# Packing the last layer's key ends over two heads, and giving GpSimd every fourth rest of the weights

## The chip, the cores and the metric

The kernel runs on one core of a Trainium2 chip. The metric is the device time of one execution in microseconds; lower is better. The same times are shown for several executions, and one execution was taken by the hardware profiler, whose trace is read below. Engines are written as in the profile: PE is TensorE's matmuls and PEld its weight loads, DVE is VectorE, ACT is ScalarE, POOL is GpSimd, SP is SyncE.

## The reference

Two transformer-like blocks for one sequence of 256 tokens and 2048 features, everything in float32. The first block is attention over compressed, selected and windowed keys beside a gated spatial unit. The second has 16 further tokens in front (272 in all) and two layers. Its even layer runs a state-space scan in both directions and a depthwise convolution of 31 taps over 2048 channels; its odd layer is neighbourhood attention on a grid:

```python
def even_layer(h, ...):
    u = rmsnorm(h, norm_g)
    z_a, xs, Bm, Cm, dt_f, dt_b, z_b, glu_v, glu_g = split(u @ w_in)
    y_a = ssd_mixer(xs, Bm, Cm, dt_f, dt_b, z_a, ...)        # conv of 5 taps, scan, gate, norm
    y_b = conformer_conv(glu_v, glu_g, ...) * silu(z_b)      # GLU, depthwise conv of 31 taps, layer norm
    return h + concat(y_a, y_b) @ w_out

def odd_layer(h, ...):
    q, k, v, z = split(rmsnorm(h, norm_g) @ w_in)
    # 32 heads of 64. A query sees 16 grid columns around its own and the 16 tokens in front
    o = softmax(q k^T / 8 + bias, masked) v
    return h + (o * silu(z)) @ w_out
```

## The kernel before

**Weights in two parts.** Products with weights keep float32's precision on a faster matmul form. `load_piece` (L89 to L101) fetches 1024 columns of weights (`raw`, on SP's queue). ACT rounds them to `wh` (L98), and DVE computes what is left, `wl = raw - wh` (L99). `raw`, `wh` and `wl` have four buffers each. Activations are split the same way, and `mm3` (L118 to L122) adds three products. `proj` (L137) makes one output block of 128 rows from 16 chunks, which are two pieces: 48 matmuls over 256 or 272 columns, 24 for each piece.

**The even layer** (`layer_e`, its projections from about 860 to 1555 us in the trace) makes 96 projections, in this order: 32 for the GLU, 16 for B and C, 16 for x, 16 for the gate z_a, 16 for z_b; of the GLU's, the first four need no split. DVE does the convolution: 480 taps, each one `scalar_tensor_tensor` on a whole channel block (L842), on SBUF alone. For 11 of the 16 blocks the taps read their inputs from the tile `early`, whose space is taken over, block by block, by `xt` when x is made; the taps on a part must be done before that. GpSimd adds the finished blocks (`vsum`, L849) and, later, the squares (L204). While B, C and x run, DVE also does the small convolution (`cacc`, L873, its input in PSUM) and then the decay tiles `m` of the scan (L904, on SBUF), which PE multiplies (`yps`, L940 and L956). DVE's gate products (`za`, L992) read PSUM.

**The odd layer** (`layer_o`) is a loop of 16 steps of two heads each: projections q, k, v and z; four transposes of v (L1154); scores for two tiles of 128 queries against 176 keys, with both heads side by side (`sp`, 352 columns); softmax on DVE and ACT; then, per tile, four transposes of the probabilities `pt_ps` (128 and 48 keys for each head, L1188 and L1189) and four products with the values (L1195, contracting 128 or 48 keys, 64 output rows for each head). Each of these products is two passes in the trace.

**What sets the order.** The program is handed to a scheduler with its own model of the engines; it puts each engine's instructions into one queue, worked off in order. `K.hook` (called at L100) and `tc.issue_after` tie taps behind the `wl` of a piece.

Of the kernel before, what the change touches and what calls it, by code (L numbers as in the profile page):

```python
# [10 lines left out]
F32 = mybir.dt.float32  # L11
# [34 lines left out]
class Core:  # L46


    def __init__(self, tc, ctx):
        self.tc, self.nc = tc, tc.nc  # L50
        nc = self.nc
        self.cp = ctx.enter_context(tc.tile_pool(name="const", bufs=1))
        self.wp = ctx.enter_context(tc.tile_pool(name="w", bufs=2))
        self.sm = ctx.enter_context(tc.tile_pool(name="small", bufs=4))
        self.ps = ctx.enter_context(tc.tile_pool(name="ps", bufs=3, space=PSUM))
        self.dr = ctx.enter_context(tc.tile_pool(name="dram", bufs=1, space=DRAM))
        self.hpool = ctx.enter_context(tc.tile_pool(name="h", bufs=1))
# [32 lines left out]
    def load_piece(self, src):  # L90
# [7 lines left out]
        nc.scalar.activation(wh, raw, AF.Copy)  # L98
        ins = nc.vector.tensor_tensor(wl, raw, wh.bitcast(F32), op=ALU.subtract)  # L99
        self.hook(ins.ins)  # L100
        return wh, wl  # L101
# [576 lines left out]
def layer_e(K, a):  # L678
# [3 lines left out]
    with ExitStack() as ctx:  # L682
# [55 lines left out]
        def glu():  # L738
# [354 lines left out]
def layer_o(K, a, out):  # L1093
# [4 lines left out]
    h = K.h  # L1098
    KR = [(0, 176), (96, T2)]
    VR = [(0, 128), (128, 176), (96, 224), (224, T2)]  # L1100
    with ExitStack() as ctx:
# [26 lines left out]
        for i in range(2):  # L1128
            nc.gpsimd.memset(kbd[i].bitcast(F32), 0.0)

        for i in range(16):
            bias = wk.tile([P, 2, 2, 176], F32, tag="bias", name="bias")
            nc.sync.dma_start(bias, a["rpb"][i])
# [14 lines left out]
            vp = K.proj(a["o_w_in"][4 * i + 2], UH, UL, T2)  # L1148
            vf = k1("vf")
            nc.vector.tensor_tensor(vf, vp, rb, op=ALU.mult)  # L1150
            vt_ps = K.ps.tile([P, 4, P], F32, tag="t", bufs=2, name="vt_ps")
            vt = wk.tile([P, 4, P], F32, tag="vt", name="vt")
            for j, (s0, s1) in enumerate(VR):
                nc.tensor.transpose(vt_ps[: s1 - s0, j, :], vf[:, s0:s1], K.ident)  # L1154
            nc.scalar.activation(vt[:, 0::2, :], vt_ps[:, 0::2, :], AF.Copy)
            nc.scalar.activation(vt[:48, 1::2, :], vt_ps[:48, 1::2, :], AF.Copy)
            zp = K.proj(a["o_w_in"][4 * i + 3], QH, QL, S)
# [8 lines left out]
            for t in range(2):  # L1166
                ts = slice(128 * t, 128 * t + 128)
                k0, k1_ = KR[t]
                K.mm3(sp[:, t, :352].rearrange("p (g k) -> p g k", g=2), qh[:, ts], ql[:, ts],
                      kb[:, 0, :, k0:k1_], kb[:, 1, :, k0:k1_], True, True)  # L1170
            sb = wk.tile([P, 2, 2, 176], F32, tag="sb", name="sb")
            nc.vector.tensor_tensor(sb.rearrange("p t g k -> p t (g k)"), sp[:, :, :352],
                                    bias.rearrange("p t g k -> p t (g k)"), op=ALU.add)
# [9 lines left out]
            for t in range(2):  # L1183
                ts = slice(128 * t, 128 * t + 128)
                pt_ps = K.ps.tile([P, 2, 2, P], F32, tag="t", bufs=2, name="pt_ps")
                for g in range(2):
                    nc.vector.tensor_scalar(sb[:, t, g], sb[:, t, g], rs[:, t, g : g + 1], None, op0=ALU.mult)
                    nc.tensor.transpose(pt_ps[:, 0, g, :], sb[:, t, g, 0:128], K.ident)  # L1188
                    nc.tensor.transpose(pt_ps[:48, 1, g, :], sb[:, t, g, 128:176], K.ident)  # L1189
                pt = wk.tile([P, 2, 2, P], F32, tag="pt", name="pt")  # L1190
                nc.scalar.activation(pt[:, 0], pt_ps[:, 0], AF.Copy)
                nc.scalar.activation(pt[:48, 1], pt_ps[:48, 1], AF.Copy)
                for kt, n in ((0, 128), (1, 48)):
                    for g in range(2):
                        nc.tensor.matmul(o_ps[64 * g : 64 * g + 64, ts], vt[:n, 2 * t + kt, 64 * g : 64 * g + 64], pt[:n, kt, g, :],  # L1195
                                         start=kt == 0, stop=kt == 1, skip_group_check=True)
            o = k1("oz", S)
# [51 lines left out]
def prep(inp):  # L1249
# [70 lines left out]
    rpb = g["o_rpb_2"][0]  # L1320
    bias = np.zeros((32, P, 2, 176), f32)
    for t, (q0, k0) in enumerate(((0, 0), (144, 96))):
        qr, qc = row[q0 : q0 + 128, None], col[q0 : q0 + 128, None]
        kr, kc = row[None, k0 : k0 + 176], col[None, k0 : k0 + 176]
        st = np.clip(qc - 8, 0, 48)
        ok = (kc >= st) & (kc < st + 16)
        b = rpb[:, np.clip(kr - qr + 7, 0, 14), np.clip(kc - qc + 15, 0, 30)]
        bias[:, :, t] = np.where(kc < 0, f32(0), np.where(ok, b, f32(-1e30)))
    o["rpb"] = np.ascontiguousarray(bias.reshape(16, 2, P, 2, 176).transpose(0, 2, 3, 1, 4))

# [49 lines left out]
```

## Time and profile before

| | us |
|---|---|
| median of 3 runs (lowest, highest) | 2284.5 (2283.99, 2286.28) |
| the profiled execution's own time | 2284.89 |
| its span in the trace | 2283.1 |
| PE busy | 2229.3 |
| DVE busy | 1628.3 |
| ACT busy | 1164.8 |
| POOL busy | 124.7 |

The span runs from the first to the last instruction; the execution's own time is 1.8 us longer. An engine's busy time is the union of its instructions. PE is busy 98% of the span, so the places of interest are those where it is not, and its own instructions where it is.

### The profile page before, as it was taken

The numbers are of one execution on the slowest core, as the hardware profiler recorded it, in microseconds if no ns is written. First come the engines' busy times: TensorE is split into PE (matmuls) and PEld (weight loads), VectorE is DVE, ScalarE is ACT, GpSimd is POOL, SyncE is SP. The second block draws the span as 40 slices with busy tenths as digits, with TensorE's granted clock in tenths as the row PEclk, the third lists the DMA queues.
The fourth block names the chain that finished last, engine by engine and source line by source line (L and its number), as shares of the span: only waits on it lengthen the run. The fifth ranks groups of instructions, "written<-read, shape, count | busy, mean of one in ns | idle before, by whom it ended". The sixth has DMA issues, their size and how long they took to land.

```text
span 2283.1 us, 44200 instructions
## 1 busy us (share of the span) xinstructions
PE 2229.3 (98%) x17798; PEld 2159.0 (95%) x17798; DVE 1628.3 (71%) x2840; ACT 1164.8 (51%) x2087; POOL 124.7 (5%) x119
## 2 busy tenths in 40 slices
PE   8999999999999999999998998899999999999997
PEld 6998799999999998999998998899999999999997
DVE  6567777555555669999999888798766555565554
ACT  4446644444444444445547887745444545454453
POOL 1000000000000130000000010002011000000011
PEclk9999999999999999999999999999999999999999
DMA  7642455555556555554554555354655555545453
GB/s 260 226 153 94 133 191 183 187 186 186 187 195 209 183 165 195 198 175 166 177 175 145 171 172 189 120 177 153 202 176 188 170 168 169 169 162 167 159 174 121
DMA packets 126413, 398.20 MB, mean 174 GB/s; under 512 B 16832, under 2 KB 33664, under 8 KB 125696
## 3 DMA queue, kind: packets, MB, share of 16 engines
q1 hardware_dynamic: 126064, 395.36, 52.5%
q8 instruction: 140, 2.29, 0.4%
q14 instruction: 65, 0.53, 0.1%
q10 hardware_dynamic: 144, 0.01, 0.0%
HBM read 390.92 MB, written 4.40 MB: 173 GB/s over the span
## 4 chain that ended last, share of the span: by engine, by line
PE 94%; DVE 3%; ACT 2%; issue 1%; DMA 0%; POOL 0%; SPq 0%; DVEq 0%; ACTq 0%; POOLq 0%
PE acc L120 29%; PE acc L122 28%; PE acc L121 28%; PE acc L156 2%; PE o_ps L1195 1%; PE yps L956 1%; DVE wl L99 1%; DVE vb L842 0%; PE pt_ps L503 0%; PE sp L120 0%; ACT wh L98 0%; PE sp L122 0%; PE sp L121 0%; PE o_ps L509 0%; DVE xin L291 0%
## 5 line engine op out<-in xcount | busy, mean ns | idle before, releaser
L98 ACT ACTIVATE wh<-raw 128x1024 fp32r<-128x1024 f32 x674 | 713.2, 1059 | 967.9 <-PE acc L121 575.6
L99 DVE TENSOR_TENSOR wl<-raw,wh 128x1024 fp32r<-128x1024 f32 x674 | 828.9, 1231 | 383.7 <-ACT wh L98 376.2
L120 PE MATMUL acc<-uh,wh 128*128 128x272 f32 (+1 forms) x1488 | 437.8, 294 | 15.7 <-DVE za L992 8.7
L122 PE MATMUL acc<-uh,wl 128*128 128x272 f32 (+1 forms) x1488 | 437.5, 294 | 0.0
L121 PE MATMUL acc<-ul,wh 128*128 128x272 f32 (+1 forms) x1488 | 435.1, 292 | 0.0
L121 PE MATMUL acc<-xl,wh 128*128 128x256 f32 (+1 forms) x1136 | 322.3, 284 | 0.0
L120 PE MATMUL acc<-xh,wh 128*128 128x256 f32 (+1 forms) x1136 | 322.2, 284 | 0.0
L122 PE MATMUL acc<-xh,wl 128*128 128x256 f32 (+1 forms) x1136 | 321.2, 283 | 0.0
L120 PEld LDWEIGHTS acc<-uh,wh 128*128 128x128 f32 (+1 forms) x1488 | 282.7, 190 | 21.5 <-DVE za L992 9.5
L121 PE MATMUL acc<-oul,wh 128*128 128x256 f32 (+1 forms) x1024 | 294.4, 287 | 0.0
L122 PE MATMUL acc<-ouh,wl 128*128 128x256 f32 (+1 forms) x1024 | 294.0, 287 | 0.0
L120 PE MATMUL acc<-ouh,wh 128*128 128x256 f32 (+1 forms) x1024 | 292.8, 286 | 0.0
L122 PEld LDWEIGHTS acc<-uh,wl 128*128 128x128 f32 (+1 forms) x1488 | 282.1, 190 | 3.5 <-issue 2.3
L121 PEld LDWEIGHTS acc<-ul,wh 128*128 128x128 f32 (+1 forms) x1488 | 282.4, 190 | 1.7 <-issue 0.8
L120 PEld LDWEIGHTS acc<-xh,wh 128*128 128x128 f32 (+1 forms) x1136 | 213.8, 188 | 1.2 <-DVE pj L316 0.4
L122 PEld LDWEIGHTS acc<-xh,wl 128*128 128x128 f32 (+1 forms) x1136 | 214.4, 189 | 0.2
L121 PEld LDWEIGHTS acc<-xl,wh 128*128 128x128 f32 (+1 forms) x1136 | 213.6, 188 | 0.7 <-issue 0.4
L122 PEld LDWEIGHTS acc<-ouh,wl 128*128 128x128 f32 x1024 | 192.6, 188 | 2.6 <-issue 2.6
L121 PEld LDWEIGHTS acc<-oul,wh 128*128 128x128 f32 x1024 | 192.7, 188 | 0.2
L120 PEld LDWEIGHTS acc<-ouh,wh 128*128 128x128 f32 x1024 | 192.8, 188 | 0.0
L842 DVE SCALAR_TENSOR_TENSOR vb<-early,par,vb 128x257 f32<-128x257 f32 (+9 forms) x330 | 148.4, 493 | 0.9 <-ACT vb L826 0.7
L204 POOL TENSOR_TENSOR sq<-sq 128x272 f32<-128x272 f32 (+1 forms) x44 | 48.5, 1103 | 747.5 <-ACT sq L201 746.7
(413 smaller groups left out, 4290.7 us busy)
## 6 DMA issues: line engine op xcount, KB each, us to landing
raw<-in_e_w_in SPq DMA_DIRECT2D x184, 512.0 KB, 4.0
raw<-in_w_in_fm SPq DMA_DIRECT2D x140, 512.0 KB, 3.9
raw<-in_o_w_in SPq DMA_DIRECT2D x128, 512.0 KB, 4.1
raw<-in_e_w_out SPq DMA_DIRECT2D x64, 512.0 KB, 4.5
raw<-in_w_up SPq DMA_DIRECT2D x32, 512.0 KB, 3.9
raw<-in_w_out SPq DMA_DIRECT2D x32, 512.0 KB, 4.4
raw<-in_w_pg SPq DMA_DIRECT2D x32, 512.0 KB, 3.8
raw<-in_o_w_out SPq DMA_DIRECT2D x32, 512.0 KB, 4.5
```

Source lines behind the costliest of these rows:

```text
L98: nc.scalar.activation(wh, raw, AF.Copy)
L99: ins = nc.vector.tensor_tensor(wl, raw, wh.bitcast(F32), op=ALU.subtract)
L120: mm(out, lh, rh, start=start, stop=False)
L121: mm(out, lh, rl, start=False, stop=False)
L122: mm(out, ll, rh, start=False, stop=stop)
L156: self.nc.tensor.matmul(a, raws[c // 8][:, c % 8, :], x(c), start=c == 0, stop=c == 15)
L204: self.nc.gpsimd.tensor_tensor(acc, acc, sq, op=ALU.add)
L842: ins = nc.vector.scalar_tensor_tensor(v[:, lo:hi], u[:, lo + o : hi + o], par(K, "e_dw_w", 31 * b + k), v[:, lo:hi], op0=ALU.mult, op1=AL ...
L956: prev = nc.tensor.matmul(o, w, m, start=False, stop=k >= 6, skip_group_check=True).ins
L1195: nc.tensor.matmul(o_ps[64 * g : 64 * g + 64, ts], vt[:n, 2 * t + kt, 64 * g : 64 * g + 64], pt[:n, kt, g, :], start=kt == 0, stop=kt == 1 ...
```

## The change

There are two independent parts.

1. **Even layer.** A counter of pieces and a `share` are added to the core. From the GLU's first projection to the end of z_b's `share` is 4, and every fourth piece's subtraction is issued to GpSimd in place of DVE. 46 pieces are concerned. The hook is then given the last subtraction that DVE did.
2. **Odd layer.** The two query tiles see 192 keys in place of 176, from 0 and from 80. Keys 128 columns wide are used for each head as its own part (from 0 for the first head and from 64 for the second), and the 64 that are left of each head are packed beside each other into one tile of 128. That makes three transposes of the probabilities per tile, and three products: one that contracts the packed tile for both heads at once (128 output rows, with a block-diagonal value tile `vb`), and one of 128 keys for each head. The scores are 384 columns wide.

```diff
@@ load_piece
         nc.scalar.activation(wh, raw, AF.Copy)
-        ins = nc.vector.tensor_tensor(wl, raw, wh.bitcast(F32), op=ALU.subtract)
-        self.hook(ins.ins)
+        self.pieces += 1
+        if self.share and self.pieces % self.share == 0:
+            nc.gpsimd.tensor_tensor(wl, raw, wh.bitcast(F32), op=ALU.subtract)
+        else:
+            self.last_wl = nc.vector.tensor_tensor(wl, raw, wh.bitcast(F32), op=ALU.subtract).ins
+        self.hook(self.last_wl)
@@ layer_e
+        K.share = 4
         early = big.tile([P, 3 * D], F32, tag="e6", name="early")
         us = [glu()]
...
         K.hook = lambda ins: None
+        K.share = 0
@@ layer_o
-    KR = [(0, 176), (96, T2)]
-    VR = [(0, 128), (128, 176), (96, 224), (224, T2)]
+    KR = [(0, 192), (80, T2)]
...
-            vf = k1("vf")
-            nc.vector.tensor_tensor(vf, vp, rb, op=ALU.mult)
+            vb = vbd[i % 2]
+            vf = k1("vf", 208)
+            for g in range(2):
+                gs = slice(64 * g, 64 * g + 64)
+                nc.vector.tensor_tensor(vf[gs], vp[gs, 64 * g : 64 * g + 208], rb[gs, 64 * g : 64 * g + 208], op=ALU.mult)
+                nc.vector.tensor_tensor(vb[gs, :, gs], two(vp[gs], 128 - 128 * g), two(rb[gs], 128 - 128 * g), op=ALU.mult)
...
-            for j, (s0, s1) in enumerate(VR):
-                nc.tensor.transpose(vt_ps[: s1 - s0, j, :], vf[:, s0:s1], K.ident)
-            nc.scalar.activation(vt[:, 0::2, :], vt_ps[:, 0::2, :], AF.Copy)
-            nc.scalar.activation(vt[:48, 1::2, :], vt_ps[:48, 1::2, :], AF.Copy)
+            for t, (k0, k1_) in enumerate(KR):
+                nc.tensor.transpose(vt_ps[:, 2 * t, :], vf[:, 80 * t : 80 * t + P], K.ident)
+                nc.tensor.transpose(vt_ps[:, 2 * t + 1, :], vb[:, t, :], K.ident)
+            nc.scalar.activation(vt, vt_ps, AF.Copy)
...
-                    nc.tensor.transpose(pt_ps[:, 0, g, :], sb[:, t, g, 0:128], K.ident)
-                    nc.tensor.transpose(pt_ps[:48, 1, g, :], sb[:, t, g, 128:176], K.ident)
-                pt = wk.tile([P, 2, 2, P], F32, tag="pt", name="pt")
-                nc.scalar.activation(pt[:, 0], pt_ps[:, 0], AF.Copy)
-                nc.scalar.activation(pt[:48, 1], pt_ps[:48, 1], AF.Copy)
-                for kt, n in ((0, 128), (1, 48)):
-                    for g in range(2):
-                        nc.tensor.matmul(o_ps[64 * g : 64 * g + 64, ts], vt[:n, 2 * t + kt, 64 * g : 64 * g + 64], pt[:n, kt, g, :],
-                                         start=kt == 0, stop=kt == 1, skip_group_check=True)
+                    nc.tensor.transpose(pt_ps[:, g, :], sb[:, t, g, 64 * g : 64 * g + P], K.ident)
+                nc.tensor.transpose(pt_ps[:, 2, :], sb[:, t].rearrange("p g k -> p (g k)")[:, 128:256], K.ident)
+                pt = wk.tile([P, 3, P], F32, tag="pt", name="pt")
+                nc.scalar.activation(pt, pt_ps[:, 0:3], AF.Copy)
+
+                nc.tensor.matmul(o_ps[:, ts], vt[:, 2 * t + 1, :], pt[:, 2, :], start=True, stop=False, skip_group_check=True)
+                for g in range(2):
+                    nc.tensor.matmul(o_ps[64 * g : 64 * g + 64, ts], vt[:, 2 * t, 64 * g : 64 * g + 64], pt[:, g, :],
+                                     start=False, stop=True, skip_group_check=True)
```

The bias tile and the tile `sb` grow from 176 to 192 keys, and two `vb` tiles are cleared on GpSimd at the layer's start.

The order of DVE in the GLU's stretch, before, from the 26th to the 29th piece after the first one that the change concerns (`wl` a piece's rest, `vb<-early` taps, `early<-gt,acc` a GLU output):

```order
L99 TENSOR_TENSOR wl<-raw,wh 128x1024
L842 SCALAR_TENSOR_TENSOR vb<-early,par,vb 128x258
L751 SCALAR_TENSOR_TENSOR early<-gt,acc 128x272
L842 SCALAR_TENSOR_TENSOR vb<-early,par,vb 128x257 x4
L99 TENSOR_TENSOR wl<-raw,wh 128x1024
L842 SCALAR_TENSOR_TENSOR vb<-early,par,vb 128x258 x2
L842 SCALAR_TENSOR_TENSOR vb<-early,par,vb 128x259
L99 TENSOR_TENSOR wl<-raw,wh 128x1024
L842 SCALAR_TENSOR_TENSOR vb<-early,par,vb 128x259
L842 SCALAR_TENSOR_TENSOR vb<-early,par,vb 128x260 x2
L842 SCALAR_TENSOR_TENSOR vb<-early,par,vb 128x261
L99 TENSOR_TENSOR wl<-raw,wh 128x1024
```

The same four pieces in the order after; the third of them is the moved one, between the second and the third `wl`:

```order
L104 TENSOR_TENSOR wl<-raw,wh 128x1024
L848 SCALAR_TENSOR_TENSOR vb<-early,par,vb 128x265
L756 SCALAR_TENSOR_TENSOR early<-gt,acc 128x272
L848 SCALAR_TENSOR_TENSOR vb<-early,par,vb 128x265
L848 SCALAR_TENSOR_TENSOR vb<-early,par,vb 128x266
L104 TENSOR_TENSOR wl<-raw,wh 128x1024
L848 SCALAR_TENSOR_TENSOR vb<-early,par,vb 128x266
L848 SCALAR_TENSOR_TENSOR vb<-early,par,vb 128x267 x2
L848 SCALAR_TENSOR_TENSOR vb<-early,par,vb 128x268 x2
L848 SCALAR_TENSOR_TENSOR vb<-early,par,vb 128x269 x2
L848 SCALAR_TENSOR_TENSOR vb<-early,par,vb 128x270 x2
L848 SCALAR_TENSOR_TENSOR vb<-early,par,vb 128x271 x2
```

Behind these rows stands the next `wl`. In the place of the moved `wl` stand taps, 11 between two rows of `wl` where there were three and four.

The order of POOL in the even layer, before (`vsum` the sum of finished convolution blocks, `sq` sums of squares, `tmp` the sum at the layer's end):

```order
L847 COPY vsum<-vb 128x272
L849 TENSOR_TENSOR vsum<-vsum,vb 128x272 x10
L204 TENSOR_TENSOR sq<-sq 128x272 x11
L849 TENSOR_TENSOR vsum<-vsum,vb 128x272 x2
L204 TENSOR_TENSOR sq<-sq 128x272 x4
L849 TENSOR_TENSOR vsum<-vsum,vb 128x272 x3
```

And after, the beginning of the same stretch:

```order
L102 TENSOR_TENSOR wl<-raw,wh 128x1024 x3
L853 COPY vsum<-vb 128x272
L102 TENSOR_TENSOR wl<-raw,wh 128x1024 x3
L855 TENSOR_TENSOR vsum<-vsum,vb 128x272 x2
L102 TENSOR_TENSOR wl<-raw,wh 128x1024 x4
L855 TENSOR_TENSOR vsum<-vsum,vb 128x272 x2
```

The moved pieces stand between the sums of `vsum`, which wait for taps; further on they stand between the sums of `sq` as well.

The order of PE in the odd layer's loop, before, the transposes of the probabilities between two projection matmuls:

```order
L120 MATMUL acc<-ouh,wh 128x272
L1188 MATMUL pt_ps<-ident,sb 128x128
L1189 MATMUL pt_ps<-ident,sb 48x128
L1188 MATMUL pt_ps<-ident,sb 128x128
L1189 MATMUL pt_ps<-ident,sb 48x128
L1188 MATMUL pt_ps<-ident,sb 128x128
L1189 MATMUL pt_ps<-ident,sb 48x128
L1188 MATMUL pt_ps<-ident,sb 128x128
L1189 MATMUL pt_ps<-ident,sb 48x128
```

After, the products with the values, which were eight of one form (`o_ps<-pt,vt 64x128 x8`):

```order
L126 MATMUL acc<-oul,wh 128x272
L1212 MATMUL o_ps<-pt,vt 128x128
L1214 MATMUL o_ps<-pt,vt 64x128 x2
L1212 MATMUL o_ps<-pt,vt 128x128
L1214 MATMUL o_ps<-pt,vt 64x128 x2
```

Their places among the projection's matmuls stay: 22 projection matmuls stand between the transposes and these products in both.

## Rows read from the trace of the kernel before

**Rows 1.** The page: busy time, share of the span, instructions, by engine.
```profile
PE 2229.3 (98%) x17798; PEld 2159.0 (95%) x17798; DVE 1628.3 (71%) x2840; ACT 1164.8 (51%) x2087; POOL 124.7 (5%) x119
```

**Rows 2.** Busy time by window: stretch, length, engines (instructions), granted PE clock, DMA.
```profile
core 0: us, PE busy (x) PEld busy (x) DVE busy (x) ACT busy (x) POOL busy (x), PEclk, DMA share, GB/s
900.00:1200.00 300.00, 300.00 (x2378) 298.43 (x2378) 285.77 (x507) 141.99 (x199) 6.94 (x9) 0.99 0.55 182
1200.00:1220.00 20.00, 17.44 (x137) 16.28 (x136) 20.00 (x48) 15.77 (x40) 0.00 (x0) 1.00 0.44 144
1220.00:1240.00 20.00, 15.00 (x101) 13.78 (x101) 17.22 (x33) 13.17 (x35) 1.60 (x2) 0.83 0.39 122
1227.40:1232.80 5.40, 5.37 (x24) 5.37 (x25) 4.82 (x12) 3.79 (x13) 0.00 (x0) 0.51 0.51 168
1241.00:1400.00 159.00, 157.06 (x1230) 148.17 (x1229) 132.96 (x273) 129.22 (x332) 9.69 (x10) 1.00 0.55 174
...
1777.00:1804.35 27.35, 27.35 (x228) 26.48 (x227) 16.15 (x25) 13.62 (x27) 0.00 (x0) 1.00 0.53 170
```

**Rows 3.** Waits (total us, times, longest) of 900 to 1200, then of 1200 to 1240.
```profile
ACT wh L98 <- PE acc L121: 102.3, 62, 2.0
...
DVE wl L99 <- ACT wh L98: 12.8, 40, 2.0
...
PE yps L956 <- DVE m L904: 5.8, 2, 4.1
```

**Rows 4.** The page's costliest groups (busy us, mean ns | idle before), then DVE's timeline.
```profile
L98 ACT ACTIVATE wh<-raw 128x1024 fp32r<-128x1024 f32 x674 | 713.2, 1059 | 967.9 <-PE acc L121 575.6
L99 DVE TENSOR_TENSOR wl<-raw,wh 128x1024 fp32r<-128x1024 f32 x674 | 828.9, 1231 | 383.7 <-ACT wh L98 376.2
...
1228.04 2.08 DVE L842 SCALAR_TENSOR_TENSOR vb<-u,par,vb 128x259 f32<-128x259 f32 x5
1230.05 0.43 DVE L880 SCALAR_TENSOR_TENSOR xs<-ct,cacc 128x272 f32<-128x272 f32 x1
```

**Rows 5.** Timeline (start, length) of DVE and POOL; L1083 by source, ns min/median/max.
```profile
1655.67 1.23 DVE L99 TENSOR_TENSOR wl<-raw,wh 128x1024 fp32r<-128x1024 f32 x1 [0.22 <-ACT wh L98]
1656.81 1.00 DVE L1083 SCALAR_TENSOR_TENSOR oul<-h,par,ouh 128x272 fp32r<-128x272 f32 x1
...
1656.44 1.07 POOL L1089 TENSOR_TENSOR tmp<-tmp,sq 128x272 f32<-128x272 f32 x1 [93.97 <-ACT sq L1088]
...
L1083 DVE SCALAR_TENSOR_TENSOR oul<-h,par,ouh x16: 494/1005/1011, 1650.7 to 1741.0; 128x272 fp32r<-128x272 f32 x16
```

**Rows 6.** L291 by source; timeline of POOL and of DVE beside it.
```profile
L291 DVE TENSOR_SCALAR xin<-xin,par x16: 340/350/1455, 4.4 to 23.1; 128x256 f32<-128x256 f32 x16
...
7.74 1.26 POOL L289 TENSOR_TENSOR sq<-sq,sq 128x512 f32<-128x512 f32 x1 [6.80 <-ACT sq L287]
...
1460.45 0.77 POOL L204 TENSOR_TENSOR sq<-sq 128x272 f32<-128x272 f32 x1 [15.48 <-ACT sq L201]
...
1460.62 0.44 DVE L992 SCALAR_TENSOR_TENSOR za<-zt,acc 128x272 f32<-128x272 f32 x1 [0.19 <-ACT zt L991]
```

**Rows 7.** Timeline of one step of the odd layer's loop, PE and (1798.18) DVE.
```profile
1791.21 0.33 PE L120 MATMUL sp<-kb,qh 128*128 128x352 f32 x1
1791.38 0.33 PE L121 MATMUL sp<-kb,qh 128*128 128x352 f32 x1
...
1798.18 0.97 DVE L1187 TENSOR_SCALAR sb<-sb,rs 128x176 f32<-128x176 f32 x4
...
1801.00 0.27 PE L1188 MATMUL pt_ps<-ident,sb 128*128 128x128 f32 x1
...
1801.76 0.27 PE L1189 MATMUL pt_ps<-ident,sb 128*48 128x128 f32 x1
...
1804.71 1.54 PE L1195 MATMUL o_ps<-pt,vt 128*64 128x128 f32 x16
1806.18 0.40 PE L122 MATMUL acc<-ouh,wl 128*128 128x272 f32 x1
```

More of the change, by code (lines that the diff above doesn't have):

```diff
@@ L60, in __init__ @@
         self.hook = lambda ins: None
+        self.share, self.pieces = 0, 0
         self.wide, self.wide_i, self.wide_t = False, 0, None
@@ L1129, in layer_o, with two @@
             nc.gpsimd.memset(kbd[i].bitcast(F32), 0.0)
+        vbd = [big.tile([P, 2, P], F32, tag="vb%d" % i, name="vb%d" % i) for i in range(2)]
+        for i in range(2):
+            nc.gpsimd.memset(vbd[i], 0.0)
+        def two(v, o):
+            v = v[:, o : o + 64]
+            return bass.AP(tensor=v.tensor, offset=v.offset, ap=[v.ap[0], [80, 2], [1, 64]])
         for i in range(16):
-            bias = wk.tile([P, 2, 2, 176], F32, tag="bias", name="bias")
+            bias = wk.tile([P, 2, 2, 192], F32, tag="bias", name="bias")
             nc.sync.dma_start(bias, a["rpb"][i])
@@ L1168, in layer_o @@
                 k0, k1_ = KR[t]
-                K.mm3(sp[:, t, :352].rearrange("p (g k) -> p g k", g=2), qh[:, ts], ql[:, ts],
+                K.mm3(sp[:, t, :384].rearrange("p (g k) -> p g k", g=2), qh[:, ts], ql[:, ts],
                       kb[:, 0, :, k0:k1_], kb[:, 1, :, k0:k1_], True, True)
-            sb = wk.tile([P, 2, 2, 176], F32, tag="sb", name="sb")
-            nc.vector.tensor_tensor(sb.rearrange("p t g k -> p t (g k)"), sp[:, :, :352],
+            sb = wk.tile([P, 2, 2, 192], F32, tag="sb", name="sb")
+            nc.vector.tensor_tensor(sb.rearrange("p t g k -> p t (g k)"), sp[:, :, :384],
                                     bias.rearrange("p t g k -> p t (g k)"), op=ALU.add)
@@ L1184, in layer_o @@
                 ts = slice(128 * t, 128 * t + 128)
-                pt_ps = K.ps.tile([P, 2, 2, P], F32, tag="t", bufs=2, name="pt_ps")
+                pt_ps = K.ps.tile([P, 4, P], F32, tag="t", bufs=2, name="pt_ps")
                 for g in range(2):
                     nc.vector.tensor_scalar(sb[:, t, g], sb[:, t, g], rs[:, t, g : g + 1], None, op0=ALU.mult)
-                    nc.tensor.transpose(pt_ps[:, 0, g, :], sb[:, t, g, 0:128], K.ident)
-                    nc.tensor.transpose(pt_ps[:48, 1, g, :], sb[:, t, g, 128:176], K.ident)
-                pt = wk.tile([P, 2, 2, P], F32, tag="pt", name="pt")
-                nc.scalar.activation(pt[:, 0], pt_ps[:, 0], AF.Copy)
-                nc.scalar.activation(pt[:48, 1], pt_ps[:48, 1], AF.Copy)
-                for kt, n in ((0, 128), (1, 48)):
-                    for g in range(2):
-                        nc.tensor.matmul(o_ps[64 * g : 64 * g + 64, ts], vt[:n, 2 * t + kt, 64 * g : 64 * g + 64], pt[:n, kt, g, :],
-                                         start=kt == 0, stop=kt == 1, skip_group_check=True)
+                    nc.tensor.transpose(pt_ps[:, g, :], sb[:, t, g, 64 * g : 64 * g + P], K.ident)
[6 more added lines that the diff above has]
+                                     start=False, stop=True, skip_group_check=True)
             o = k1("oz", S)
@@ L1320, in prep @@
     rpb = g["o_rpb_2"][0]
-    bias = np.zeros((32, P, 2, 176), f32)
-    for t, (q0, k0) in enumerate(((0, 0), (144, 96))):
+    bias = np.zeros((32, P, 2, 192), f32)
+    for t, (q0, k0) in enumerate(((0, 0), (144, 80))):
         qr, qc = row[q0 : q0 + 128, None], col[q0 : q0 + 128, None]
-        kr, kc = row[None, k0 : k0 + 176], col[None, k0 : k0 + 176]
+        kr, kc = row[None, k0 : k0 + 192], col[None, k0 : k0 + 192]
         st = np.clip(qc - 8, 0, 48)
@@ L1328, in prep @@
         bias[:, :, t] = np.where(kc < 0, f32(0), np.where(ok, b, f32(-1e30)))
-    o["rpb"] = np.ascontiguousarray(bias.reshape(16, 2, P, 2, 176).transpose(0, 2, 3, 1, 4))
+    o["rpb"] = np.ascontiguousarray(bias.reshape(16, 2, P, 2, 192).transpose(0, 2, 3, 1, 4))
     o["c_ident"] = np.eye(P, dtype=f32)
```

## The prediction

> **What bounds the kernel now.** The busy table comes first: TensorE is busy for 2229.3 of 2283.1 us [rows 1], so 54 us of its idle time are all that less waiting can give, and apart from that only less work on TensorE can. Next come the windows of the second block, one row for each stretch, where the reader is to compare PE with DVE [rows 2]. From 900 to 1200 us PE is busy for all 300 us, and VectorE for 285.77: it has 14.2 us to spare in 300. From 1200 to 1240 us PE idles 2.56 and 5.00 us while VectorE is busy for all of the first 20; the waits of that stretch name VectorE's `m` [rows 3]. After it PE runs at a granted clock of 0.51, the lower of its two levels (1.2 GHz), from 1227.4 to 1232.8 us: 24 matmuls in 5.4 us, where the 900 to 1200 row (2378 matmuls in 300 us) makes 24 of them 3.0 us. So that stall costs 7.6 + 2.4 = 10 us. From 1241 to 1400 us PE idles only 1.9 us of 159, and VectorE 26. In the last layer a step of its loop takes 27.35 us and PE is busy for all of it: that loop is TensorE's own work.
>
> How far does VectorE run ahead of TensorE? ACT's `wh` waits for PE to release a buffer (62 times from 900 to 1200 us), and `wl` waits for `wh` [rows 3]. With four buffers a piece is begun when PE has finished the piece four before it. PE takes 24 x 0.126 = 3.0 us for a piece, so it needs the new one 9 us later; 1.06 us of `wh` and 1.23 of `wl` [rows 4] leave a lead of **6.8 us**. VectorE may fall that far behind before PE waits.
>
> **The pieces on GpSimd.** 46 of the second block's pieces move. Each takes one `wl` off VectorE, which from start to start is worth 1.14 us (1655.67 to 1656.81) [rows 5]. GpSimd's own time for 1024 columns is not in the trace. 512 columns take 1.26 us and 272 take 0.77 [rows 6]; the line through both gives 2.3 us for 1024. That alone would be harmless, as GpSimd is almost free.
>
> The price is what VectorE does meanwhile. `L1083` reads two SBUF tensors; undisturbed it takes 494 ns, and 1005 in the median, when a GpSimd sum of 272 columns runs beside it [rows 5]: it loses 0.51 us. `L291`, a scalar operation on SBUF, goes from 350 to 1455 ns beside a GpSimd sum of 512 columns [rows 6]: 1.1 us lost. An operation that reads PSUM loses nothing: `L992` takes 0.44 us in the middle of a GpSimd sum [rows 6]. So VectorE stands still for nearly the whole GpSimd operation as soon as it comes to one on SBUF alone, and both `wl` and the taps of the convolution are of that kind. For 1024 columns: twice the 512 row is 2.2 us, 1024/272 of the 272 row is 1.9, GpSimd's whole 2.3 is the upper end. I take **2.1 us**, near the 512 row. A moved piece then saves VectorE 1.14 us and costs it 2.1.
>
> The Trainium skill, page "SBUF — State Buffer", section "SBUF: two separate sides", says that the port pair shared by the two engines is an exclusive lock for the whole instruction, against a VectorE operation with two SBUF inputs too. The rows agree in kind but show a little less than the whole: 0.51 us of a 0.77 us sum. By the page a piece would cost the full 2.3 us, and the 23 pieces counted below 5 us more than I take.
>
> **Where it falls.** The new order of VectorE does not use the freed time as slack: it fills it with taps. From the first moved piece (trace 897 us) to the `wl` of the 90th piece from there (1164 us) the order of before has 275 taps, that of after 331, its last ones that read the early buffer. A tap is 0.41 us from start to start (five of them from 1228.04 to 1230.05, [rows 4]). So, for VectorE in these 267 us: 23 pieces moved, -23 x 1.14 = -26.2 us; 56 more taps, +23.0; standing still, 23 x 2.1 = +48.3. Together **+45 us**. Against it: its idle time, 14.2 x 267/300 = 12.6 us; the lead of 6.8; and some 3 us in which it works off PSUM operations under a GpSimd piece (my choice; 0 to 8). PE is late by 45 - 12.6 - 6.8 - 3 = **+23 us** at the end of this stretch. With 1.9 us a piece it is 18, with 2.3 it is 27 or, without the PSUM cover, 30.
>
> **What comes back.** The 10 us stall at 1200 to 1240 us arises because the last taps on the early buffer must be done there before it is overwritten. In the new order they have all gone by then, so I take it as recovered: **-10 us** (0 to -10).
>
> **The rest of the second block** has the other 23 moved pieces. Some 10 of them fall between 1241 and 1400 us, and add 10 x (2.1 - 1.14) = 10 us of VectorE to a stretch in which it idles 26: no new bound. But a decay tile `m` that stands behind a GpSimd piece is up to 2.1 us late, and PE's queue waits for it in order; so do the sums of GpSimd itself, which now stand between its pieces. Bounds: 0, as the 16 sums of `sq` on GpSimd there today leave PE only 1.9 us idle [rows 2], and 23 x 0.6 = 14. I take **+5 us**, nearer to that row.
>
> **The last layer.** Per step PE loses two of eight transposes of the probabilities: eight start 0.109 us apart (1801.00 to 1801.76 in seven intervals), -0.22 us. The product with the values goes from 16 passes in 1.47 us (0.092 each, 1804.71 to 1806.18) to eight of the same form and four with a full 128 columns of weights, for which the nearest row is the transposes' 0.109 [rows 7]: 1.17, -0.30 us. At the other end a full product costs as much as the pair it replaces, and nothing is saved. The six score matmuls grow from 352 to 384 columns: 0.17 us for 352 (1791.21 to 1791.38), so about 0.08 us more for the six. The sum is -0.44 us a step, times 16 = **-7 us** (-2 to -8). The four transposes of the values remain. VectorE's two half-height products in place of one, the 9% wider additions and ACT's longer exponentials lie beside PE: VectorE works 16.15 of 27.35 us [rows 2], and its scaled probabilities are done at 1799.15, 1.8 us before their transposes [rows 7]; 9% on that chain is under 0.5 us. ACT's copies become fewer. The larger bias (9% of one transfer a step) and GpSimd's two new clears are covered by the projections that run then; if not, they cost a microsecond once.
>
> **Sum.** The profiled execution took 2284.89 us, 0.4 above the median of 2284.5. 2284.9 + 23 - 10 + 5 - 7 = **2296 us**, 0.5% slower.
>
> **The rivals.** *GpSimd relieves VectorE (faster).* If a piece held VectorE for under 1.1 us, PE would never be late in the long stretch (23 x 1.1 - 26.2 + 23.0 is 22 us, the sum of idle time, lead and cover), the stall at 1200 would still go, and the time would be 2284.9 - 10 - 7 = 2268. For it: there are 22 us of room, and most sums on GpSimd today cost PE nothing. Against it: the rows show 1.1 us for half the size already. Below 1.6 us a piece the whole change is a gain.
>
> *It evens out.* With 1.6 to 1.8 us a piece, or with more PSUM work under the pieces, PE is 11 to 16 us late, and after -10, +5 and -7 the time is 2284 to 2289. For it: lead and idle time are my estimates, a few microseconds each.
>
> *The queues make it worse.* GpSimd's sums of `vsum` wait for taps, and pieces stand behind them in its queue; with late taps these pieces come late as well, each `m` is late, and the stall at 1200 is not recovered. With 2.3 us a piece: 2284.9 + 28 - 3 + 12 - 6 = 2316. Against it: the pieces behind a sum are three to four ahead of what PE then needs.
>
> *The layer's edit gives nothing*: if full products cost what the pairs did, it is 2 us in place of 7, and 2301.
>
> **How the numbers follow.** Chances: forecast and its neighbours (2290 to 2308) 0.50; worse 0.15; evens out 0.17; faster 0.18. A measurement of this kernel can tell about 0.2% (4.6 us) from no change, so below 2280 is faster and above 2289 slower: faster 0.18, same 0.17, slower 0.65. The range leaves out about one in ten at either end: 2275, between the relief and the even case, to 2316, the worse one. The likeliest case's own range is 2290 to 2308.
>
> **What would show it.** In the new profile GpSimd's 46 operations of 1024 columns should take 2.3 us or more; beside them single `wl` and taps should show 2 to 3 us where they take 1.2 and 0.5 today. VectorE should be busy for all but a few of the 300 us from 900 to 1200, PE should idle there for the first time (some 20 us, released by `wl`), and the gap at 1200 to 1240 should be gone. In the last layer a step should take 26.9 us. I am wrong if `wl` and taps keep their lengths beside GpSimd, or if PE still has no idle time before 1160 us.

## The result and the profile after

The changed kernel takes 2297.39 us in the median of four runs (2296.52 to 2299.23), the kernel before 2284.24 beside it (2283.06 to 2286.28). The ratio is **1.0058, with a 95% interval of 1.004 to 1.0075**: slower. The prediction was 2296 (2275 to 2316). The profiled execution took 2297.27 us, with a span of 2294.9 where it was 2283.1.

The page's busy table of the changed kernel, to be read against [rows 1]:

```profile
PE 2227.8 (97%) x17702; PEld 2156.7 (94%) x17702; DVE 1666.9 (73%) x2842; ACT 1154.6 (50%) x2037; POOL 255.3 (11%) x167
```

VectorE lost 46 instructions of 1.23 us (57 us) and yet is busy for 38.6 us more. The last layer's part adds 13.8 of these (1642.1 us in `layer_alone`, where the pieces stay on VectorE); the other 25 come with the pieces. The windows of the second block and of one step of the last layer, as in [rows 2] (stretch, length, busy time of each engine, granted clock, DMA):

```profile
900.00:1200.00 300.00, 283.18 (x2200) 278.12 (x2200) 299.47 (x489) 122.14 (x171) 74.09 (x34) 0.99 0.49 166
1200.00:1220.00 20.00, 18.49 (x142) 17.96 (x142) 15.70 (x30) 14.56 (x32) 2.39 (x1) 1.00 0.60 198
1220.00:1240.00 20.00, 20.00 (x158) 18.66 (x158) 17.06 (x33) 17.63 (x45) 2.64 (x2) 1.00 0.47 146
1240.00:1400.00 160.00, 159.07 (x1246) 149.82 (x1245) 134.71 (x252) 129.71 (x332) 36.74 (x20) 1.00 0.56 181
1804.12:1831.25 27.13, 27.13 (x222) 26.54 (x221) 17.00 (x29) 13.43 (x25) 0.00 (x0) 1.00 0.50 170
```

From 900 to 1200 us VectorE (third busy figure) has 0.5 us of idle time left of 14.2, and PE idles 16.8 us where it idled none. From 1200 to 1240 us PE idles 1.5 us in place of 7.6. A step of the last layer takes 27.13 us in place of 27.35. Who releases PE in the long stretch is told by the waits from 860 to 1200 us (total us, times, longest):

```profile
PEld acc L127 <- DVE wl L104: 18.8, 14, 3.2
PE acc L127 <- DVE wl L104: 15.7, 13, 3.0
DVE wl L104 <- ACT wh L99: 4.1, 2, 2.9
PE acc L127 <- POOL wl L102: 1.6, 2, 0.8
```

VectorE's `wl` ends nearly all of PE's waits; GpSimd's own `wl` ends 1.6 us. VectorE itself waits for `wh` twice, where [rows 3] had 40 times: the lead is gone.

Why VectorE is late stands in the groups. First GpSimd's pieces, then the taps on the early buffer and VectorE's pieces (ns: least, median, most):

```profile
L102 POOL TENSOR_TENSOR wl<-raw,wh x46: 2342/2514/4217, 895.5 to 1537.4; 128x1024 fp32r<-128x1024 f32 x46
...
L848 DVE SCALAR_TENSOR_TENSOR vb<-early,par,vb x330: 366/486/2641, 879.9 to 1175.2; 128x257 f32<-128x257 f32 x11, 128x259 f32<-128x259 f32 x11, 128x261 f32<-128x261 f32 x11, 128x263 f32<-128x263 f32 x11
...
L104 DVE TENSOR_TENSOR wl<-raw,wh x628: 957/1225/3412, 26.0 to 2269.7; 128x1024 fp32r<-128x1024 f32 x156, 128x768 fp32r<-128x768 f32 x1
```

The median tap and the median piece keep their lengths; single ones take 2.6 and 3.4 us. The timeline shows which (start, length; VectorE, then GpSimd):

```profile
942.18 1.23 DVE L104 TENSOR_TENSOR wl<-raw,wh 128x1024 fp32r<-128x1024 f32 x1
943.32 2.64 DVE L848 SCALAR_TENSOR_TENSOR vb<-early,par,vb 128x269 f32<-128x269 f32 x1
...
943.14 2.52 POOL L102 TENSOR_TENSOR wl<-raw,wh 128x1024 fp32r<-128x1024 f32 x1 [10.65 <-ACT wh L99]
```

The GpSimd piece runs from 943.14 to 945.66. The `wl` already running at its start ends normally; the tap that starts 0.18 us after it ends at 945.96, 0.3 us after GpSimd. So it is beside 40 of the 46 pieces: one VectorE operation on SBUF alone is held until the piece has ended, a tap until 0.3 us after it, a `wl` until 1.1 us after it. Beside the other six none is held. The contrast, an operation with PSUM input under a piece:

```profile
1210.91 2.10 DVE L879 SCALAR_TENSOR_TENSOR cacc<-acc,par,cacc 128x270 f32<-128x270 f32 x4 [0.97 <-ACT cacc L875]
...
1210.48 2.39 POOL L102 TENSOR_TENSOR wl<-raw,wh 128x1024 fp32r<-128x1024 f32 x1 [12.03 <-ACT wh L99]
```

Four `cacc`, which read PSUM, take 2.10 us as they do elsewhere: that piece cost VectorE nothing. Summed over all pieces (each VectorE operation that overlaps one, its length less the median of its own kind where GpSimd is still), the loss is 81.0 us, 1.76 us for each of 46.

What a late piece costs PE, seen at the worst place (VectorE's piece held by a GpSimd one from 970.15 to 972.69, then PE):

```profile
970.40 3.37 DVE L104 TENSOR_TENSOR wl<-raw,wh 128x1024 fp32r<-128x1024 f32 x1
...
973.83 0.59 PE L127 MATMUL acc<-uh,wl 128*128 128x272 f32 x1 [2.98 <-DVE wl L104]
974.22 0.43 PE L125 MATMUL acc<-uh,wh 128*128 128x272 f32 x1
974.45 0.43 PE L126 MATMUL acc<-ul,wh 128*128 128x272 f32 x1
...
973.80:978.00 4.20, 4.17 (x18) 4.17 (x19) 4.20 (x11) 0.00 (x0) 0.00 (x0) 0.50 0.70 226
```

PE idles 2.98 us, and behind that its matmuls start 0.23 us apart in place of 0.126, at a granted clock of 0.50. In the whole stretch 178 matmuls are missing against before (2378 less 2200), 22.4 us at 0.126: 16.8 of them are idle time. The lower clock is a small part of the rest: 6.8 us of the stretch ran at 0.50, where the kernel before had 3.4 (17 matmuls in 3.40 us), which makes under 2 us. Most of the rest does not show as idle time because a matmul's record is 0.29 us long while the next one starts after 0.126, so that a wait looks some 0.16 us shorter than it is, and a shorter one does not show at all.

### The profile page after: what moved, and what is told of

Read it like the earlier page. It is cut to its first block, busy times and chain, and to the rows that moved or that the text cites. A ratio compares the mean times of both kernels' runs of the same rounds, so it can differ in the third digit from the quotient of the medians.

```text
span 2294.9 us, 43991 instructions
## 1 busy us (share of the span) xinstructions
PE 2227.8 (97%) x17702; PEld 2156.7 (94%) x17702; DVE 1666.9 (73%) x2842; ACT 1154.6 (50%) x2037; POOL 255.3 (11%) x167
## 4 chain that ended last, share of the span: by engine, by line
PE 82%; DVE 14%; issue 1%; ACT 1%; DMA 1%; POOL 0%; SPq 0%; DVEq 0%; ACTq 0%; POOLq 0%
PE acc L125 25%; PE acc L127 25%; PE acc L126 25%; DVE vb L848 7%; DVE wl L104 3%; DVE cacc L879 1%; PE yps L962 1%; PE acc L161 1%; PE o_ps L1214 1%; PE pt_ps L508 0%; PE sp L125 0%; PE sp L127 0%; PE sp L126 0%; PE o_ps L1212 0%; PE o_ps L514 0%
## 5 line engine op out<-in xcount | busy, mean ns | idle before, releaser
L104 DVE TENSOR_TENSOR wl<-raw,wh 128x1024 fp32r<-128x1024 f32 x628 | 779.1, 1242 | 388.8 <-ACT wh L99 384.8
L125 PE MATMUL acc<-uh,wh 128*128 128x272 f32 (+1 forms) x1488 | 438.1, 294 | 10.5 <-DVE za L998 6.8
L848 DVE SCALAR_TENSOR_TENSOR vb<-early,par,vb 128x257 f32<-128x257 f32 (+9 forms) x330 | 189.8, 626 | 1.0 <-ACT vb L832 0.7
L102 POOL TENSOR_TENSOR wl<-raw,wh 128x1024 fp32r<-128x1024 f32 x46 | 121.8, 2649 | 416.0 <-ACT wh L99 398.7
```

Source lines behind the costliest of these rows:

```text
L102: nc.gpsimd.tensor_tensor(wl, raw, wh.bitcast(F32), op=ALU.subtract)
L104: self.last_wl = nc.vector.tensor_tensor(wl, raw, wh.bitcast(F32), op=ALU.subtract).ins
L125: mm(out, lh, rh, start=start, stop=False)
L848: ins = nc.vector.scalar_tensor_tensor(v[:, lo:hi], u[:, lo + o : hi + o], par(K, "e_dw_w", 31 * b + k), v[:, lo:hi], op0=ALU.mult, op1=AL ...
```

## The experiments

Lateness in this section is read at the start of ACT's `wh` of a given piece, counted from the program's first: its time less that of the kernel before, less the same difference at the 260th piece (830 us), which is ahead of the change. It runs some three pieces ahead of PE (9 us), and where this lead shrinks `wh` is later than PE itself. Where PE's own lateness is meant, the same projection matmul by its place in PE's order is compared, counted from the one at 860 us: in the changed kernel the matmuls that the kernel before starts at 1164, 1199, 1240 and 1660 us are 23.4, 26.9, 16.5 and 15.4 us late.

| piece (time before) | 300 (988) | 360 (1174) | 380 (1254) | 420 (1410) | 490 (1658) |
|---|---|---|---|---|---|
| the change | +9.6 | +27.8 | +20.9 | +13.3 | +15.4 |
| `relief_wh` | -0.2 | +3.6 | -1.5 | -10.5 | -10.3 |
| `lock_no_relief` | +11.2 | +30.8 | +37.3 | +37.9 | +37.9 |
| `share_early` | +9.5 | +24.7 | +13.8 | +7.9 | +13.6 |
| `share_late` | -0.2 | -0.3 | +6.3 | +2.7 | +7.9 |
| `share6_layer` | +2.8 | +10.2 | +8.1 | +6.4 | +8.4 |
| `share8_layer` | +0.8 | +2.9 | -7.0 | -1.9 | +3.5 |
| `share16_layer` | -0.1 | -0.2 | -4.0 | -5.3 | -2.8 |
| `taps_later` | 0.0 | +0.9 | -9.8 | -1.5 | -0.3 |

**The two parts apart.**

```diff
-        K.share = 4
+        K.share = 0
```

> The last layer's edit alone; no piece goes to GpSimd. From the trace of the changed kernel: the first product with the values of the first and of the last step of the loop lie 407.4 us apart in place of 411.0, 0.24 us less for each of 15 intervals, so 16 x 0.24 = 3.8 us and 2284.2 - 3.8 = 2280.4 (ratio 0.998). The prediction's term was -7, which would give 2277 (0.997). Rival: the changed loop is shorter only because it follows a late layer, and alone it gains nothing: 2284 (1.000).

> Every fourth piece on GpSimd in the second block, the last layer as before. If the two parts add up: the even layer's end lay 15.4 us later in the changed kernel's trace (last sums of squares at 1759.4 in place of 1744.0), so 2284.2 + 15.4 + 0.4 = 2300 (1.007). The prediction's terms (+23 - 10 + 5) would give 2302. Rival: the later end of the even layer is partly made good in the last layer, and the part alone costs less than 12 us: below 2296.

Measured: the layer's edit 2279.28 us, ratio 0.9977 (0.9967 to 0.9986); GpSimd's part 2302.18, ratio 1.0076 (1.006 to 1.0091). The parts add up: 0.9977 x 1.0076 = 1.0053, and the whole change has 1.0058. Each step of the layer takes 27.13 us in the run of its own as well, so 16 x 0.22 = 3.5 us are its own; the ratio's 5 us hold these within their interval.

**Standing still, or the order, or GpSimd's queue?** Two kernels take the pieces' relief and their lock apart. In the first no engine computes the moved rests. In the second VectorE computes everything, and GpSimd computes the rests of 27 pieces once more, into unused space.

```diff
-            nc.gpsimd.tensor_tensor(wl, raw, wh.bitcast(F32), op=ALU.subtract)
+            wl = wh
```

> As the run with the GpSimd part alone, but the rest of the 46 pieces is computed by no engine: the third product of each of these pieces takes the rounded weights once more (so that part of the computation is left out). VectorE's order is nearly the same, with the taps in the place of the moved pieces, but nothing of theirs runs on GpSimd. If the standing still beside GpSimd is the price: VectorE has -23 x 1.14 + 56 x 0.41 = -3 us in the long stretch, PE is never late there, the stall at 1200 to 1240 us goes, and the time is 2284 - 10 = 2274 (0.9955). Rival, the order is the price (taps put ahead of the pieces make the pieces late): PE still idles before 1200 us, 2290 or more (above 1.002).

```diff
         ins = nc.vector.tensor_tensor(wl, raw, wh.bitcast(F32), op=ALU.subtract)
+        self.pieces += 1
+        if self.share and self.pieces % self.share == 0:
+            nc.gpsimd.tensor_tensor(self.scr[:, :n], raw, wh.bitcast(F32), op=ALU.subtract)
```

> The kernel before, with 27 GpSimd subtractions of 1024 columns added (22 up to the end of B and C, 5 beside x), each on every fourth piece's raw and rounded weights, into unused space. Nobody waits for their result; VectorE keeps all its 674 pieces, and its order moves by a few taps. If standing still is the price: 22 x 2.07 = 45.5 us of it against 22 us of idle time, lead and cover makes PE 24 us late by 1170 us, the 5 further ones add some 8 in the stretch where VectorE is already late: 2284 + 24 + 8 = 2316 (1.014; 1.010 to 1.016). Rival, the price is that pieces come late out of GpSimd's queue behind the sums: nobody waits for these, so 2284 (1.000). Rival, the order: 2284 too.

Measured: 2274.86 us, ratio 0.9957 (0.9943 to 0.9971), and 2322.09, ratio 1.0168 (1.0154 to 1.0182). The windows of the first (with a stretch at the lower clock), then of the second:

```profile
1030.80:1041.00 10.20, 10.20 (x43) 8.38 (x42) 5.03 (x12) 5.34 (x16) 0.00 (x0) 0.50 0.22 73
900.00:1200.00 300.00, 300.00 (x2342) 296.78 (x2342) 272.46 (x519) 143.16 (x206) 13.18 (x11) 0.98 0.55 178
1200.00:1240.00 40.00, 40.00 (x320) 38.19 (x319) 29.27 (x60) 34.64 (x88) 0.00 (x0) 1.00 0.56 179
```

```profile
900.00:1200.00 300.00, 280.04 (x2175) 274.78 (x2175) 299.70 (x454) 123.41 (x172) 78.37 (x32) 0.99 0.50 166
1200.00:1240.00 40.00, 33.51 (x253) 31.80 (x253) 40.00 (x72) 18.53 (x34) 5.48 (x2) 1.00 0.48 158
```

With the changed order and nothing on GpSimd PE never idles up to 1240 us, and the stall is gone for good (-10.3 at the 490th piece). The +3.6 us at the 360th piece are no wait: from 1030.8 to 1041.0 us PE ran without a gap at a granted clock of 0.50, where the kernel before had 3.4 us of it. So the taps moved ahead cost no idle time. With the lock alone, and nobody who waits for GpSimd's result, PE idles 20 us in the long stretch and VectorE is busy without a gap. So the price is the standing still; neither the order nor late results of GpSimd are needed for it. The second run is 6 us above what was expected. Up to 1170 us it did as expected: PE's matmul there is 25.6 us late, for 24. (`wh`, at +30.8, is later because the lead is gone.) The miss lies behind: up to the end PE loses 11 to 12 us more, where the five further pieces were put at 8.

**How many pieces?** The same kernel with every sixth, eighth and sixteenth piece.

```diff
-        K.share = 4
+        K.share = 8
```

> Every sixteenth piece on GpSimd (12 in all), the last layer's edit kept. Up to the first x projection 6 pieces are moved and 16 more taps stand in VectorE's order: -6.8 + 6.6 + 12.4 = +12 us, within the 22 us, so PE is not late; but 16 of the 32 early taps that stand beside x before are still there, so only about half of the stall goes, -5; the last layer -4. Theory: 2276 (0.996). Rival, a fixed price per piece: a quarter of +17, with the layer 2285 (1.000).

> The changed kernel with every eighth piece on GpSimd in place of every fourth (23 in all), the last layer's edit kept. Up to the first x projection VectorE's order has 12 pieces moved and 30 more taps than the kernel before: -12 x 1.14 + 30 x 0.41 + 12 x 2.07 = +23.4 us against the 22 us of idle time, lead and cover, so PE is some 2 us late; all taps on the early buffer stand ahead of the second x, so the stall at 1200 to 1240 goes, -10; the last layer gives -4. Theory (a price per piece and a budget of 22 us): 2285 + 2 - 10 - 4 = 2273 (0.995; 0.993 to 0.9965), faster than the kernel before and than the last layer's edit alone (0.998). Rival, each moved piece costs the same whatever their number: half of +17, with the layer 2289 (1.002).

> Every sixth piece on GpSimd (31 in all), the last layer's edit kept. Up to the first x projection 16 pieces are moved, and 42 more taps stand in VectorE's order: -18.2 + 17.2 + 33.1 = +32 us against 22: PE is 10 us late; the stall goes, -10; the last layer -4. Theory: 2281 (0.998). Rival, a fixed price per piece: two thirds of +17, with the layer 2292 (1.003).

Measured: 2277.83 us, ratio 0.9977 (0.9968 to 0.9986); 2284.41, 1.0003 (0.9994 to 1.0012); 2286.23, 1.0014 (1.0004 to 1.0024). The layer's edit alone has 0.9977: so the sixteenth gives nothing measurable, the eighth costs 6 us and the sixth 8. Both theories missed. The budget held in the long stretch: net loads of 12, 23 and 32 us made PE -0.2, +2.9 and +10.2 us late at the 360th piece (expected 0, 2 and 10). It failed behind it: the eighth was 7.0 us ahead at the 380th piece, as expected, and gave back 10.5 us by the 490th. The pattern over the runs with GpSimd or moved taps is that the earlier PE comes out of the stall, the more it loses behind it: from PE's matmul at 1240 us of the time before to the one at 1660, `share8_layer` goes from -7.7 to +3.6, `taps_later` (below) from -8.5 to -0.3, `share6_layer` from +3.5 to +8.5, `share_early` from +14.0 to +13.6. The reading is that VectorE is not there yet when PE comes early; no run shows it by itself. The waits of `share8_layer` from 1240 to 1400 us:

```profile
PE acc L125 <- DVE cacc L879: 3.4, 3, 1.4
```

The kernel before has one such wait of 1.9 us there. The rest of what is given back, after 1400 us, was not traced to one wait.

**Early and late pieces apart.** GpSimd's share ends, or begins, with x.

```diff
+        K.share = 0    # or 4
         K.hook = lambda ins: tap(TAPS[2], ins)
```

> The changed kernel, but GpSimd gets every fourth piece only up to the end of B and C (22 of the 46); from x on VectorE does all pieces. VectorE's order up to x stays that of the changed kernel. The prediction gave the rest of the second block +5 us: without it 2297.4 - 5 = 2292 (1.0035). Rival, by the changed kernel's trace (PE 31 us late at the 370th piece, 20 at the 380th, 15 at the 490th): the later pieces cost nothing, as VectorE has idle time there, and the time stays 2297 (1.006).

> The changed kernel, but GpSimd gets every fourth piece only from x on (24 pieces); before it VectorE does all. The long stretch is that of the last layer's edit alone (no lateness), and the stall at 1200 to 1240 stays, with some taps standing earlier beside x. By the prediction (+5 for the rest, nothing recovered, last layer -4): 2285.5 (1.0005). Rival, the later pieces cost nothing: as the last layer's edit alone, 2280 (0.998). If every piece costs its standing still less its relief (1.35 - 1.14 us in this stretch in the changed kernel's trace), 24 x 0.2 = 5: as the prediction.

Measured: 2295.54 us, ratio 1.0054 (1.0041 to 1.0067), and 2288.78, ratio 1.0021 (1.0012 to 1.003). Against the layer's edit alone the early pieces cost 17.5 us, the late ones 10, both together 18.5, each to within some 3 us. They don't add up. The first time lies between its two expectations, nearer to the rival, the second above both of its own. Alone, the late ones fall into the stall at 1200 to 1240 us, where VectorE is short already (the 380th piece is 6.3 us late); behind the early ones that stall has gone and PE is late, so VectorE has time for them; this last step is a reading of the table, not shown by itself. What the late ones cost inside the change is 1 to 2 us (1.8 at the 490th piece; the times alone can't tell it from nothing).

**Is the stall worth 10 us by itself?** Here its taps are moved without GpSimd (`K.share = 0`, and the products in halves, as in the last experiments below).

```diff
-TAPS = [20, 1, 0, 1, 4]
+TAPS = [18, 1, 0, 2, 4]
...
-NEARLY = 11
-NM, NK1 = 8, 6
+NEARLY = 9
+NM, NK1 = 8, 4
```

> No piece on GpSimd; the last layer's edit with the packed product in halves (2275.5 in its own run, 0.996); and the cause of the stall at 1200 to 1240 us taken away in another manner: 9 blocks of the convolution in place of 11 read the early buffer (the other 7 have tiles of their own, paid for with two buffers less of the k1 tiles), all their 270 taps stand before x in VectorE's order, and 44 taps of the others in place of the 12 + 60, so that 28 taps move from beside x into the z_a stretch, where VectorE idles 26 us of 159. If the stall is VectorE's taps before that deadline, it goes without any standing still: 2275.5 - 10 = 2265.5 (0.992). Rivals: the taps are late in the z_a stretch or the fewer k1 tiles stall it, and it gives the gain back: 2275 (0.996) or above.

Measured: 2273.33 us, ratio 0.996 (0.9946 to 0.9973); the same kernel without this edit has 0.9961. The rival was right. The windows, and the wait that took the stall's place (1240 to 1480 us; the kernel before has 8.7 us of it, in two waits):

```profile
1200.00:1240.00 40.00, 39.18 (x312) 36.97 (x312) 32.52 (x63) 35.69 (x92) 0.00 (x0) 1.00 0.57 171
1240.00:1400.00 160.00, 152.88 (x1174) 142.40 (x1172) 142.63 (x293) 123.64 (x316) 12.71 (x12) 0.99 0.55 170
...
PE acc L125 <- DVE za L998: 15.1, 4, 5.6
```

PE is 9.8 us ahead at the 380th piece and has lost it by the 490th, where the taps now stand. The stall is where VectorE's debt showed; moved work shows elsewhere. Of the runs here only the one with less work on VectorE, `relief_wh`, keeps the 10 us. That two buffers fewer play a part was not ruled out.

**The products with the values.** First PE's timeline in the changed kernel, the projection's last matmul before them, the products of a step and the next projection matmul (x counts passes):

```profile
1819.45 0.29 PE L126 MATMUL acc<-oul,wh 128*128 128x272 f32 x1
1819.58 0.38 PE L1212 MATMUL o_ps<-pt,vt 128*128 128x128 f32 x2
1819.89 0.44 PE L1214 MATMUL o_ps<-pt,vt 128*64 128x128 f32 x4
1820.26 0.49 PE L1212 MATMUL o_ps<-pt,vt 128*128 128x128 f32 x2
1820.68 0.44 PE L1214 MATMUL o_ps<-pt,vt 128*64 128x128 f32 x4
1821.05 0.39 PE L127 MATMUL acc<-ouh,wl 128*128 128x272 f32 x1
```

Twelve passes take 1.47 us, as sixteen did [rows 7]. Two kernels ask whether it is the full product that is dear.

```diff
-                nc.tensor.matmul(o_ps[:, ts], vt[:, 2 * t + 1, :], pt[:, 2, :], start=True, stop=False, skip_group_check=True)
+                for g in range(2):
+                    nc.tensor.matmul(o_ps[64 * g : 64 * g + 64, ts], vt[:, 2 * t + 1, 64 * g : 64 * g + 64], pt[:, 2, :],
+                                     start=True, stop=False, skip_group_check=True)
```

> The last layer's edit alone, with the packed keys' product made as two products of 64 output rows each in place of one of 128 rows (same sums). If a full product costs as much as the pair that it replaced (the trace of the changed kernel shows the eight products of a step in 1.47 us, as before): a step stays at 27.13 us, and the time equals that of the layer's edit alone, 2279 to 2281 (0.998). By the prediction's term (full products at 0.109 us, 0.30 us saved a step) it would be 16 x 0.3 = 4.8 us longer: a step of 27.4 us, 2285 (1.000).

> The last layer's edit alone, the six products of a step in another order: the two full ones first (one projection matmul stands between them), then the four of 64 rows, where the order was full, two halves, full, two halves. The instructions are the same. In the traces the first pass behind a change between 128 and 64 columns of weights starts 0.20 to 0.21 us after the one before, a pass behind one of its own form 0.10 to 0.13. If that change is the price, two of four changes go and a step takes 27.13 - 2 x 0.1 = 26.93 us, the whole 16 x 0.2 = 3 us less than the layer's edit alone: 2276 to 2277 (0.9963). Rival, a full product is dear by itself: a step stays at 27.13 us (0.9977).

Measured: 2275.51 us, ratio 0.9961 (0.9948 to 0.9974), with a step of 26.78 us; and 2274.66, ratio 0.9969 (0.9954 to 0.9984), with 26.80. (In the second kernel the second tile's first product begins while the first tile's sum in the same PSUM bank is open, which drops the first tile's packed product; it is read for its times alone.) The timelines, of the halves and of the regrouped order:

```profile
1805.48 0.29 PE L126 MATMUL acc<-oul,wh 128*128 128x272 f32 x1
1805.70 0.44 PE L1213 MATMUL o_ps<-pt,vt 128*64 128x128 f32 x4
1805.97 0.39 PE L1216 MATMUL o_ps<-pt,vt 128*64 128x128 f32 x4
1806.19 0.39 PE L1213 MATMUL o_ps<-pt,vt 128*64 128x128 f32 x4
1806.41 0.39 PE L1216 MATMUL o_ps<-pt,vt 128*64 128x128 f32 x4
1806.73 0.39 PE L127 MATMUL acc<-ouh,wl 128*128 128x272 f32 x1
```

```profile
1800.79 0.29 PE L126 MATMUL acc<-oul,wh 128*128 128x272 f32 x1
1800.91 0.38 PE L1216 MATMUL o_ps<-pt,vt 128*128 128x128 f32 x2
1801.05 0.38 PE L127 MATMUL acc<-ouh,wl 128*128 128x272 f32 x1
1801.26 0.39 PE L1216 MATMUL o_ps<-pt,vt 128*128 128x128 f32 x2
1801.58 0.66 PE L1220 MATMUL o_ps<-pt,vt 128*64 128x128 f32 x8
1802.17 0.39 PE L125 MATMUL acc<-ouh,wh 128*128 128x272 f32 x1
```

From the matmul before the products to the one after them, the changed kernel takes 1.60 us, the halves 1.25 with four passes more, the regrouped order 1.38 with a projection matmul of 0.13 in it. Neither expectation allowed for the halves being faster. The same instructions in another order are 0.33 us faster, so the change between 128 and 64 columns of weights has a price, about 0.16 us each (0.33 for two). The kernel before pays one as well: its products alternate between 128 and 48 contracted rows, and a pass behind such a change starts 0.20 us after the one before.

The packing itself gains nothing either. Without its projection matmul the regrouped order takes 1.25 us for twelve passes, the halves 1.25 for sixteen, with as many changes of form. In the trace two halves start within 0.007 us of each other, one pair 0.10 us after the last, and a full pass 0.11 us after a full one: a full product of two passes costs what its pair of halves costs, as the prediction's last rival had it.

That the halves save 0.57 us a step against the kernel before makes the layer's edit with halves, and no GpSimd, the kernel that beats both: **2275.5 us, 0.9961**.

## Why the prediction came out right, step by step

- **The price of a piece** was put at 2.1 us, from a 512-column operation [rows 6]. Over the 22 early pieces of `share_early` it is 2.06 (45.3 us in all). Over all 46 it is 1.76, since the later ones often fall on PSUM work. The held tap does last until just after GpSimd's end, as in the rows at 943 us; what the price lacks of GpSimd's 2.5 us is the tap's own length and whatever ran before it came to SBUF. The Trainium skill, page "SBUF — State Buffer", section "SBUF: two separate sides", has the lock last for the whole instruction; with GpSimd's median piece that is an estimate of 2.5 us, and the trace agrees in kind. One reading in the prediction was off: the sum beside `L1083` took 1.07 us, not 0.77 [rows 5], and 0.37 of it had passed when `L1083` started.
- **PE late by 23 us** at 1164 us: PE's matmul of that time is 23.4 us late, the first use of the 360th weights 25 (1207.8 in place of 1182.7 us). Right. The 3 us that were taken off for PSUM work belong into the price, which as measured contains them already: 23 x 2.06 us without them give 25.
- **-10 us from the stall**: PE's idle time from 1200 to 1240 us fell from 7.6 to 1.5 us with no lower clock, and `share_early` goes from 24.7 us late to 13.6, -11. Right for this change. The reason given, that the taps have gone, was not enough: `taps_later` and `share8_layer` have none of these taps there either and gave the gain back. It was kept here, where PE came late; that this is the reason is a reading of the pattern above.
- **+5 us in the rest**: 1 to 2 us inside the change (`share_early` against the whole). The term was too large, within its bounds.
- **-7 us in the last layer**: 27.13 us a step, -0.22 and not -0.44, so -3.5 us. The transposes gave their 0.22; the scores cost 1.05 us in place of 0.97 from the first to the matmul after them, the 0.08 of the sum; the products gave 0.08 with the gap ahead of them, not 0.30. The step that failed is the product's price. Its 0.092 us for a pass of 64 columns was a mean over pairs that run side by side, with the changes of form in it; a full pass follows a full one after 0.11 us in the first tile, as taken, but after 0.21 in the second, behind halves.
- Together: +25, -11, +2 and -3.5 make +12.5; the span grew by 11.8. That the forecast's +11 is so near is in part luck: the gain of the layer was overrated by 3.5 us and the cost of the rest of the block by 3, and the two cancel. The mechanism of the large term was right.
- **The rivals.** That GpSimd relieves VectorE would need a price under 1.1 us; it is 2.06. The queues: PE waits 1.6 us for GpSimd's pieces, and `lock_no_relief` is slow without any such wait. The layer's edit gives 3.5 us, between the 2 of the rival "nothing" and the term's 7; for the products alone the rival was the nearer.

## What to carry to other kernels

Before work is given to GpSimd, look at what VectorE does beside it: here an operation on SBUF alone waited for GpSimd's end, at 2.06 us for a piece that relieved VectorE of 1.14. A move like this pays only where it relieves VectorE of more than it holds it up, or where it falls on VectorE's PSUM work or idle time. A stall that an engine's backlog caused was not won by moving the backlog: follow the lateness past the stall, to the end of the block. Keep matmuls of one weight form together, and before counting passes look at which of them start together and where the form changes.

## What was not expected of the hardware

Two products of 64 output rows each, on the two halves of the array, took less time than one of 128 beside such halves: 1.25 us for sixteen passes against 1.60 for twelve. In the halves' kernel the pairs start 0.10 us apart, and a change of weight form costs about 0.16 us. The Trainium skill, page "TensorEngine Tiling (Array Packing)", section "Key Properties", says that changing the tiling mode drains TensorE. No run here shows the drain as such, but the regrouped run agrees that a change has a price.
